# Issuing the first loads of a transfer-bound LoRA kernel ahead of the opening barrier, and its weights from a second queue

## The chip, the cores and the metric

The kernel runs on one core of one Trainium2 chip. An instruction on a queue (SP's or ACT's) issues a transfer, and the core's 16 DMA engines carry it out; the profile records each piece that an engine moves as a packet. The time is the device time of that core in microseconds (us), median of several executions. The *span* of a profile, from the first to the last instruction, is some 1.7 us shorter than the device time (163.3 against 165.0), so differences of spans can be read as differences of time.

## The reference

```python
x: (16, 2048, 256) f32   W: (256, 256)   lora_A: (256, 16)   lora_B: (16, 256)   lora_E: (16,)   scale = 1.0
x_flat = x.reshape(-1, 256)                                  # 32768 rows
y = x_flat @ W + scale * ((x_flat @ lora_A) * lora_E) @ lora_B
```

33.55 MB of x are read and 33.55 MB of y are written; the weights are 0.29 MB.

## The kernel before

The program is written engine by engine with semaphores. It folds the low-rank part into one matrix, `weff = W + A·diag(E)·B`, and then makes one matmul per tile. x comes in 8 chunks of 4 MB, each held in one of six SBUF homes of 128 partitions x 32 rows; y overwrites x in its home and is stored from there. SP issues all transfers, in one fixed order.

```python
LOAD_PIECES = {0: [8, 8, 16]}          # chunk 0 is loaded in three pieces
ORDER = ["L0", ..., "L5", "S0", "S1", "L6", "L7", "S2", ..., "S7"]
# ... cut ...
def sync_program():
    def load(pc):
        c, s, e = pc
        if c >= N_HOMES:
            sync.wait_ge(stored_of[c - N_HOMES], 16)
        sync.dma_start(out=home(c)[:, s:e, :], in_=x_chunks[c, :, s:e, :]).then_inc(loaded[pc], 16)

    load(pieces[0])                                     # 1 MB
    for name, to, of in (("w", ...), ("a", ...), ("e", ...), ("b", ...)):
        sync.dma_start(out=to[:], in_=of).then_inc(set_up_loaded[name], 16)
    for step in ORDER[:-1]:
        ...                                             # loads; stores wait for s_chunk
        if c == EARLY_AFTER:                            # after the load of chunk 1
            sync.wait_ge(s_first, 1)                    # a first small store of 2 KB
            sync.dma_start(out=y_chunks[0, :16, 0, :32], in_=home(0)[:16, 0, :32]).then_inc(s_early, 16)
# ... gpsimd: cast to bf16; tensor: transpose and multiply; scalar, vector: evict ...
nc.sync.dma_start(out=y_chunks[last], in_=home(last)[:])   # the last store
```

The whole program begins with a barrier of all engines: each drains and reports, GpSimd gathers the reports after setting some constants (at 0.5 to 0.6 us in the profile), and all are released (SP at 0.66 us).

## Time and profile before

| | before |
|---|---|
| time, median of 3 | 164.98 us (164.93 to 165.04) |
| span | 163.3 us |
| bytes moved | 67.4 MB |
| busiest compute engine (PE) | 61% of the span |
| first data packet of x | 1.97 us |
| last data packet ends | 161.83 us |

First, three lines of the page of the kernel before: busy tenths of PE and of the 16 DMA engines, and GB/s, in 40 slices of 4.1 us.

```profile
PE   0399948999999999999930089999960000000000
...
DMA  5999999998998998999999999999999999999990
GB/s 165 411 452 458 393 498 393 409 490 385 466 433 385 490 385 379 417 425 468 409 442 433 409 450 425 427 433 442 417 450 409 450 425 433 442 425 433 450 393 16
```

The DMA engines are busy in all slices but the first and the last; PE has holes, and is idle for the last quarter. GB/s jumps from slice to slice because a 32 KB packet is counted whole in one slice (the window from 58 to 60 us has a busy share of 1.39). So I read it over long windows. The last two columns of this view are the DMA engines' mean busy share and GB/s.

```profile
core 0: us, PE busy (x) PEld busy (x) DVE busy (x) ACT busy (x) POOL busy (x), PEclk, DMA share, GB/s
0.00:2.00 2.00, 0.00 (x0) 0.00 (x0) 0.00 (x0) 1.10 (x1) 0.70 (x6) 1.00 0.02 4
2.00:4.00 2.00, 0.00 (x0) 0.00 (x0) 0.00 (x0) 0.19 (x1) 0.00 (x0) 1.00 0.95 311
...
24.00:58.00 34.00, 32.57 (x268) 27.79 (x268) 25.98 (x22) 22.27 (x22) 24.74 (x24) 0.95 1.00 432
...
104.00:158.00 54.00, 16.87 (x145) 13.99 (x143) 15.95 (x14) 11.38 (x12) 9.68 (x10) 0.69 1.00 431
158.00:160.00 2.00, 0.00 (x0) 0.00 (x0) 0.00 (x0) 0.00 (x0) 0.00 (x0) 0.50 0.57 246
```

The rate is 432 GB/s while PE is busy for 33 of 34 us, and 431 from 120 to 150 us, where it is busy for 1.0 of 30: compute does not set it. 67.4 MB / 432 GB/s are 156 us of the 163.3. The only large stretch in which the DMA engines have nothing to do is the first 2 us (share 0.02). SP's issues show why.

```profile
0.94 0.38 SPq L106 DMA_DIRECT2D home<-in_x_dram  x1
1.38 0.42 SPq L115 DMA_DIRECT2D w_sb<-in_W_dram  x1
1.85 0.42 SPq L115 DMA_DIRECT2D a_sb<-in_lora_A_dram  x1
2.32 0.65 SPq L115 DMA_DIRECT2D e_sb<-in_lora_E_dram  x1
3.02 0.41 SPq L115 DMA_DIRECT2D b_sb<-in_lora_B_dram  x1
3.47 1.38 SPq L106 DMA_DIRECT2D home<-in_x_dram  x3
14.45 0.35 SPq L125 DMA_DIRECT2D out_dram<-home  x1
```

The first load is issued at 0.94 us (start, then duration), because SP has to pass the opening barrier (released at 0.66 us), and its first packet moves 1.03 us later. After that, transfers are issued well before their turn: the store of chunk 0 at 29.13 us. At the other end, SP waits 39.3 us for the last store:

```profile
SPq L272 <- DMA out_dram<-home: 39.3, 1, 39.3
```

### The profile page before, as it was taken

How to read it: one execution, taken by the hardware profiler on the slowest of the kernel's cores; microseconds unless marked ns; L12 is line 12 of the kernel's file. 1: busy time of each engine (PE TensorE's matmuls, PEld its weight loads, DVE VectorE, ACT ScalarE, POOL GpSimd, SP SyncE). 2: the span in 40 equal slices, each digit the busy share in tenths (PEclk: the TensorE clock that was granted, in tenths of full speed). 3: DMA queues.
4: the chain of work that ended last, by engine and by line, in shares of the span. 5: the costliest groups of instructions: out<-in, count | busy, mean ns of one | idle time of the engine just before them, and what ended most of it. 6: DMA issues, size and time to landing. Idle time of an engine off the chain costs nothing. (4 is left out here: it accounts for less than half of the span.)

```text
span 163.3 us, 2148 instructions
## 1 busy us (share of the span) xinstructions
PE 99.2 (61%) x778; PEld 82.6 (51%) x778; DVE 79.6 (49%) x66; ACT 66.1 (40%) x65; POOL 67.1 (41%) x70
## 2 busy tenths in 40 slices
PE   0399948999999999999930089999960000000000
PEld 0268837888888888888820078888840000000000
DVE  0115861788988888888850025888880000000000
ACT  3044732777767676777720025677720000000000
POOL 1444615777777677777500155677500000000000
PEclk9999995999999999999995557999996555555555
DMA  5999999998998998999999999999999999999990
GB/s 165 411 452 458 393 498 393 409 490 385 466 433 385 490 385 379 417 425 468 409 442 433 409 450 425 427 433 442 417 450 409 450 425 433 442 425 433 450 393 16
DMA packets 2979, 67.43 MB, mean 413 GB/s; under 512 B 528, under 2 KB 544, under 8 KB 672
## 3 DMA queue, kind: packets, MB, share of 16 engines
q1 hardware_dynamic: 2976, 67.41, 96.8%
q14 instruction: 3, 0.02, 0.0%
HBM read 33.85 MB, written 33.56 MB: 413 GB/s over the span
## 5 line engine op out<-in xcount | busy, mean ns | idle before, releaser
L181 DVE COPY home<-psum_y 128x1024 f32<-128x1024 f32 x64 | 78.4, 1225 | 32.8 <-PE psum_y L204 30.0
L151 POOL CAST stage<-home 128x1024 bf16<-128x1024 f32 x64 | 66.4, 1041 | 48.8 <-PE psum_xt L196 24.8
L162 ACT COPY xt<-psum_xt 128x1024 bf16<-128x1024 bf16 x64 | 64.8, 1012 | 52.7 <-PE psum_xt L196 52.7
L204 PE MATMUL psum_y<-weff,xt 128*128 128x256 bf16 x512 | 70.2, 283 | 1.0
L204 PEld LDWEIGHTS psum_y<-weff,xt 128*128 128x128 bf16 x512 | 48.3, 101 | 14.7 <-issue 7.1
L196 PE MATMUL psum_xt<-ident,stage 128*128 128x128 f32 x260 | 42.6, 290 | 14.0 <-PEq L189 14.0
L196 PEld LDWEIGHTS psum_xt<-ident,stage 128*128 128x128 f32 x260 | 33.2, 151 | 16.1 <-issue 15.1
L216 PE MATMUL psum_y<-ident,a_sb 128*16 128x128 f32 x2 | 0.6, 396 | 6.8 <-DMA a_sb<-in_lora_A_dram 6.8
L167 DVE TENSOR_SCALAR ate<-psum_y,e_sb 16x256 f32<-16x256 f32 x1 | 0.5, 471 | 7.5 <-PE psum_y L216 7.5
L216 PEld LDWEIGHTS psum_y<-ident,a_sb 128*16 128x16 f32 x2 | 0.1, 90 | 6.8 <-issue 6.8
L222 PE MATMUL psum_y<-b_sb,ate 16*128 16x256 f32 x4 | 2.1, 666 | 0.0
L177 DVE TENSOR_TENSOR weff<-w_sb,psum_y 128x512 bf16<-128x512 f32 x1 | 0.7, 689 | 2.4 <-PE psum_y L222 2.4
L162 ACT ACT_TABLE_LOAD x1 | 1.3, 1283 | 0.9 <-SPq L230 0.9
L222 PEld LDWEIGHTS psum_y<-b_sb,ate 16*128 16x128 f32 x4 | 1.2, 318 | 0.5 <-issue 0.3
L133 POOL MEMSET ident<- 128x128 f32 x1 | 0.2, 204 | 0.5 <-SPq L230 0.5
L135 POOL TENSOR_SCALAR_AFFINE_SELECT ident<-ident 128x128 f32<-128x128 f32 x1 | 0.3, 293 | 0.2 <-POOL ident L133 0.2
L258 POOL MEMSET const-float32-0.0<- 128x1 f32 x1 | 0.1, 98 | 0.2 <-issue 0.2
L258 POOL MEMSET const-bfloat16-1.0<- 128x1 bf16 x1 | 0.1, 101 | 0.0
L258 POOL MEMSET const-uint8-127<- 128x1 uint8 x1 | 0.1, 101 | 0.0
L258 POOL MEMSET const-float32-1.0<- 128x1 f32 x1 | 0.1, 98 | 0.0
## 6 DMA issues: line engine op xcount, KB each, us to landing
out_dram<-home SPq DMA_DIRECT2D x8, 4096.0 KB, 42.1
home<-in_x_dram SPq DMA_DIRECT2D x7, 4096.0 KB, 19.9
home<-in_x_dram SPq DMA_DIRECT2D x2, 1024.0 KB, 5.3
home<-in_x_dram SPq DMA_DIRECT2D x1, 2048.0 KB, 10.1
w_sb<-in_W_dram SPq DMA_DIRECT2D x1, 256.0 KB, 5.1
a_sb<-in_lora_A_dram SPq DMA_DIRECT2D x1, 16.0 KB, 4.9
e_sb<-in_lora_E_dram SPq DMA_DIRECT2D x1, 0.1 KB, 4.6
b_sb<-in_lora_B_dram SPq DMA_DIRECT2D x1, 16.0 KB, 4.0
```

Source lines behind the costliest of these rows:

```text
L133: gpsimd.memset(ident[:], 0.0).then_inc(s_ident, 1)
L135: gpsimd.affine_select(out=ident[:], in_=ident[:], compare_op=ALU.not_equal, fill=1.0, base=0, pattern=[[-1, P]], channel_multiplier=1,).t ...
L151: gpsimd.tensor_copy(out=stage[g % NS][:], in_=home(c)[:, b:b + CG, :]).then_inc(s_stage, 1)
L162: scalar.copy(out=xt[g % NX][:], in_=halves).then_inc(s_xt, 1)
L167: vector.tensor_scalar(out=ate[:], in0=psum_y[0][:R, :KT, :P], scalar1=e_sb[:], scalar2=float(scale), op0=ALU.mult, op1=ALU.mult,).then_in ...
L177: vector.tensor_add(out=weff[:], in0=w_sb[:], in1=psum_y[1][:, :KT, :]).then_inc(s_free, NY)
L181: vector.tensor_copy(out=home(c)[:, b:b + CG, :], in_=psum_y[g % NY][:]).then_inc(s_free, 1)
L196: ins = tensor.transpose(psum_xt[i % NT][:, b, :], words[:, b, :], ident[:])
L204: ins = tensor.matmul(psum_y[i % NY][:, b, :], xt[i % NX][:, b, t, :], weff[:, t, :], start=(t == 0), stop=(t == KT - 1),)
L216: ins = tensor.transpose(psum_y[0][:R, t, :P], a_sb[:, t, :], ident[:])
L222: ins = tensor.matmul(psum_y[1][:, t, :], ate[:, t, :], b_sb[:], start=True, stop=True)
L258: nc = _bacc.Bacc("TRN2", target_bir_lowering=False, num_devices=1)
```

## The change

The intent: let the transfers start earlier. The first x load and the load of A are moved, when the program is finalized, ahead of the opening barrier's drain on their engines. The four weight loads go to the scalar queue (ACT), so that SP's next instruction after the barrier is the second x load.

```diff
+    opening = []
+    def ahead_of_entry_barrier(nc):
+        ...   # take each instruction named in `opening` out of its block and
+        ...   # put it ahead of its engine's first Drain in the first block
+    nc.at_finalize(ahead_of_entry_barrier)
     def sync_program():
-        load(pieces[0])
-        for name, to, of in (("w", ...), ("a", ...), ("e", ...), ("b", ...)):
-            sync.dma_start(out=to[:], in_=of).then_inc(set_up_loaded[name], 16)
+        opening.append(load(pieces[0]).ins.name)
     def scalar_program():
+        for name, to, of in (("a", ...), ("e", ...), ("b", ...), ("w", ...)):
+            ins = scalar.dma_start(out=to[:], in_=of).then_inc(set_up_loaded[name], 16)
+            if name == "a":
+                opening.append(ins.ins.name)
         for g in range(N_GROUPS):
```

More of the change, by code (lines that the diff above doesn't have):

```diff
@@ L99 @@
     sync, gpsimd, scalar, vector, tensor = nc.sync, nc.gpsimd, nc.scalar, nc.vector, nc.tensor
+    opening = []
+    def ahead_of_entry_barrier(nc):
+        blocks = nc.main_func.blocks
+        for name in opening:
+            block = next(b for b in blocks if any(i.name == name for i in b.instructions))
+            ins = next(i for i in block.instructions if i.name == name)
+            assert not ins.sync_info.on_wait
+            block.instructions = [i for i in block.instructions if i.name != name]
+            first = blocks[0].instructions
+            at = next(
+                n for n, i in enumerate(first) if i.engine == ins.engine and isinstance(i, mybir.InstDrain)
+            )
+            blocks[0].instructions = first[:at] + [ins] + first[at:]
+    nc.at_finalize(ahead_of_entry_barrier)
     def sync_program():
@@ L105, in load @@
                 sync.wait_ge(stored_of[c - N_HOMES], 16)
-            sync.dma_start(out=home(c)[:, s:e, :], in_=x_chunks[c, :, s:e, :]).then_inc(loaded[pc], 16)
-        load(pieces[0])
-        for name, to, of in (
-            ("w", w_sb, W.rearrange("(q t) m -> q t m", t=KT)),
-            ("a", a_sb, lora_A.rearrange("(q t) r -> q t r", t=KT)),
-            ("e", e_sb, lora_E[:, None]),
-            ("b", b_sb, lora_B),
-        ):
-            sync.dma_start(out=to[:], in_=of).then_inc(set_up_loaded[name], 16)
+            ins = sync.dma_start(out=home(c)[:, s:e, :], in_=x_chunks[c, :, s:e, :])
+            return ins.then_inc(loaded[pc], 16)
+        opening.append(load(pieces[0]).ins.name)
         for step in ORDER[:-1]:
@@ L156, in scalar_program @@
     def scalar_program():
+        for name, to, of in (
+            ("a", a_sb, lora_A.rearrange("(q t) r -> q t r", t=KT)),
+            ("e", e_sb, lora_E[:, None]),
+            ("b", b_sb, lora_B),
+            ("w", w_sb, W.rearrange("(q t) m -> q t m", t=KT)),
+        ):
+            ins = scalar.dma_start(out=to[:], in_=of).then_inc(set_up_loaded[name], 16)
+            if name == "a":
+                opening.append(ins.ins.name)
         for g in range(N_GROUPS):
```

## The prediction

> **What bounds the kernel now.** The transfers. The page's DMA row is at 0.9 or above in every slice but the first and last; PE, the busiest engine, has 61% of the span. The windows give 432 GB/s from 24 to 58 us and 431 from 104 to 158: one flat rate[...]. 67.4 MB at 432 GB/s are 156 us of the 163.3 us span. The rest: about 2 us before the first packet (window 0 to 2 us: share 0.02), a slow first 2 us of data (311 GB/s), a dip when stores begin (60 to 62: 262 GB/s, partly made up around it), an uneven finish of the 16 DMA engines (158 to 160: share 0.57) and some 2 us of completion and closing barrier. Issuing is not the limit: the timeline of SP shows transfers issued well before their data moves (store of chunk 0: issued at 29, moves at about 59). Compute is off the path: the last output is issued at 122.7 us and SP then waits 39.3 us for its landing (SP's waits).
>
> **What the change does.**
> 1. The first x load (1 MB) goes ahead of the opening barrier. Before, SP's first step is at 0.0 us, this load's issue at 0.94, and packets begin at about 1.97: 1.03 us after issue. Now the issue should begin at 0.0 to 0.1 and packets near 1.1: 0.85 to 0.95 us earlier. The issue's 0.38 us fits before the barrier opens (GpSimd, with its memsets and drain, arrives last, at about 0.6), so the barrier should open as before or up to 0.1 us later. The 1 MB lasts 2.4 us at full rate, so the second x load, now SP's first after the barrier (near 1.0, packets near 2.1), follows without a gap. All transfers shift by about 0.9 us; this is the gain.
> 2. Four issues (0.42+0.42+0.65+0.41 = 1.9 us) leave SP for ACT. That alone buys nothing, since the rings had work meanwhile, but it keeps step 1 free of a gap. [...] the bytes are the same.
> 3. ACT issues e, b, W before its table load (1.28 us): done by about 4 us, its first copy was at 8.3. No cost.
> 4. Set-up: a_sb lands near 2.5 instead of 6.8 us, the first stage cast starts near 5 instead of 5.85, the early store's issue moves from 14.45 to about 13.4. None of it is on the path.
>
> **Prediction.** 164.98 - 0.9 = 164.1 us, 80% range 163.8 to 164.5. Faster by over 2%: 0.01; within 2%: 0.98; slower by over 2%: 0.01.
>
> **What would show it.** Step 1: first x issue at 0.0 to 0.1 us, window 0 to 2 us carrying 150 to 300 GB/s instead of 4, second x load issued near 1.0; 24 to 58 us unchanged at 432; span near 162.4. Step 2: a second queue of about 0.3 MB in the queue table. Step 4: early store about 1 us earlier.
>
> **What would make it wrong.** An issue before the barrier that takes longer than 1.03 us to its first packet; ACT's issue of A (0.42 us, begun at about 0.13) delaying the barrier; a gap after the first 1 MB; small weight packets from a second queue slowing x; a different tail, since the 16 engines finish over about 1.7 us; the dip at 60 us growing.

No term of the sum goes with them: it is still the time before less the shift of all transfers, 164.98 - 0.9 = 164.1 us. Three figures are rough or estimates. That the store of chunk 0 moves at about 59 us is an estimate (25.5 MB at 432 GB/s; by the packet records they have moved at 62.2 us). That a_sb lands near 2.5 us rests on no trace: the quickest landing in the trace before took 4.0 us. The "some 2 us" after the transfers are 1.45 us by the packet records. "The rings had work" rests on the window from 2 to 4 us, in which SP still issues weights and the DMA share is 0.95.

## The result

| | before | after |
|---|---|---|
| time, median (4 runs each) | 164.95 us (164.81 to 165.04) | 163.54 us (163.53 to 164.06) |
| ratio, 95% interval | | 0.9925 (0.9907 to 0.9944) |
| span | 163.3 us | 161.8 us |
| first data packet | 1.97 us | 1.01 us |
| last data packet ends | 161.83 us | 160.30 us |

Ratios here and below are the mean time of one kernel's fast runs over that of the other's fast runs of the same rounds, so not quite the ratio of the medians. The gain of the medians is 1.41 us where I had predicted 0.9; the time lies below my range (163.8 to 164.5).

The same lines of the changed kernel's page:

```profile
PE   0564999999999999999930099999940000000000
...
DMA  7999999999999999999999999999999999999991
GB/s 262 369 426 442 470 414 421 462 421 413 462 421 421 454 391 421 454 421 423 446 421 438 446 413 429 456 405 438 446 405 446 446 405 446 446 405 454 438 405 73
```

The difference is in the first slice, 262 GB/s instead of 165; the middle looks alike. The windows of the changed kernel:

```profile
0.00:2.00 2.00, 0.00 (x0) 0.00 (x0) 0.00 (x0) 0.00 (x0) 0.70 (x6) 1.00 0.46 119
2.00:4.00 2.00, 0.00 (x0) 0.00 (x0) 0.00 (x0) 1.28 (x1) 0.00 (x0) 1.00 1.00 410
...
24.00:58.00 34.00, 33.51 (x292) 28.52 (x290) 29.53 (x25) 24.43 (x25) 25.23 (x25) 1.00 1.01 434
...
104.00:158.00 54.00, 14.99 (x129) 12.43 (x128) 14.40 (x12) 10.12 (x10) 8.32 (x8) 0.66 1.00 431
158.00:160.00 2.00, 0.00 (x0) 0.00 (x0) 0.00 (x0) 0.00 (x0) 0.00 (x0) 0.50 0.12 49
```

The steady rate is the old one (434 and 431). The first window now carries data, and from 158 to 160 us there is little left to move. The issues of SP and ACT, from the timeline of the changed kernel (4 x loads merged in the first line; the second of them begins at 1.14 us):

```profile
0.00 2.42 SPq L125 DMA_DIRECT2D home<-in_x_dram  x4
0.12 0.39 ACTq L176 DMA_DIRECT2D a_sb<-in_lora_A_dram  x1
...
1.10 0.38 ACTq L176 DMA_DIRECT2D e_sb<-in_lora_E_dram  x1
...
1.51 0.45 ACTq L176 DMA_DIRECT2D b_sb<-in_lora_B_dram  x1
...
1.99 0.45 ACTq L176 DMA_DIRECT2D w_sb<-in_W_dram  x1
...
13.37 0.69 DVE L199 TENSOR_TENSOR weff<-w_sb,psum_y 128x512 bf16<-128x512 f32 x1 [6.53 <-DMA w_sb<-in_W_dram]
...
17.41 0.36 SPq L138 DMA_DIRECT2D out_dram<-home  x1
```

SP's wait for the last store is nearly what it was (39.7 us against 39.3): the whole row of transfers moved, its length didn't.

```profile
SPq L294 <- DMA out_dram<-home: 39.7, 1, 39.7
```

The first load is issued at 0.00 instead of 0.94 us. But the set-up came *later*, against my prediction: weff, made at 10.41 us before, waits for W until 13.37 us, and the first small store went from 14.45 to 17.41 us. The table of issues of the changed kernel (KB each, us from issue to landing) shows the cause:

```profile
w_sb<-in_W_dram ACTq DMA_DIRECT2D x1, 256.0 KB, 11.3
a_sb<-in_lora_A_dram ACTq DMA_DIRECT2D x1, 16.0 KB, 4.7
```

Before, on SP's queue, the same view had

```profile
w_sb<-in_W_dram SPq DMA_DIRECT2D x1, 256.0 KB, 5.1
a_sb<-in_lora_A_dram SPq DMA_DIRECT2D x1, 16.0 KB, 4.9
```

W's 128 pieces of 2 KB are 8 for each of the 16 DMA engines. In the packet records of the changed kernel one piece of W and one of x mostly follow each other: at first some 0.4 us from one piece of W to the next, with an 8 KB piece of x (0.31 us) between them, then 0.7 us, with a 16 KB piece (0.61 us). Of the 128 pieces of W, 55 begin where only a piece of x ends and 9 where only another piece of W does; for nearly all others both fit. Here an engine with work in both queues thus mostly took one piece from each in turn, and a small load on an otherwise short queue was still held up by large x pieces: the pieces of W begin between 6.41 and 12.17 us, before the change between 4.96 and 6.00. It did not put compute on the path, since the store of chunk 0, issued at 28.62 us, still comes behind 25.5 MB that have moved only by 61.1 us.

How then did a shift of 0.96 us become 1.41 to 1.5? I took the packet records (start and duration of every piece) and strung them into 16 chains, a packet following the one that ended where it starts. Each chain is one DMA engine; two that end within a few ns of each other can be exchanged, which leaves the set of 16 end times as it is. In us of the span:

| | first packet | mean end of the 16 engines | mean end - first packet | last engine behind the mean | last packet to end of span |
|---|---|---|---|---|---|
| before | 1.97 | 159.71 | 157.74 | 2.12 | 1.45 |
| after | 1.01 | 158.79 | 157.78 | 1.52 | 1.46 |

The difference of the spans, 1.52 us, is 0.96 (earlier first packet) - 0.04 + 0.60 (the last engine lags less) + 0.00. So the question is: does the change make the lag of the last engine smaller, or was that luck?

- **Theory A**: the weights on a second queue put the engines out of step, the dip in rate at the switch from loads to stores becomes shallower (window 60 to 62 us: 262 GB/s before, 377 after), the last engine loses less. Worth 0.5 us each time.
- **Theory B**: lag and dip scatter from run to run. The change is worth its shift, and my range ignored the scatter.
- **Theory C**: the earlier start itself makes the dip smaller.

### The profile page after: what moved, and what is told of

Its sections match the earlier page's. It is cut to its first block, busy times and chain, and to the rows that moved or that the text cites. A ratio compares the mean times of both kernels' runs of the same rounds, so it can differ in the third digit from the quotient of the medians.

```text
span 161.8 us, 2148 instructions
## 1 busy us (share of the span) xinstructions
PE 97.7 (60%) x778; PEld 80.9 (50%) x778; DVE 79.5 (49%) x66; ACT 66.1 (41%) x65; POOL 67.2 (42%) x70
## 3 DMA queue, kind: packets, MB, share of 16 engines
q1 hardware_dynamic: 2624, 67.11, 97.1%
## 5 line engine op out<-in xcount | busy, mean ns | idle before, releaser
L226 PE MATMUL psum_y<-weff,xt 128*128 128x256 bf16 x512 | 69.2, 280 | 4.7 <-PEq L211 3.7
L226 PEld LDWEIGHTS psum_y<-weff,xt 128*128 128x128 bf16 x512 | 47.4, 100 | 18.4 <-issue 11.1
L218 PE MATMUL psum_xt<-ident,stage 128*128 128x128 f32 x260 | 41.7, 286 | 11.2 <-PEq L211 11.2
L218 PEld LDWEIGHTS psum_xt<-ident,stage 128*128 128x128 f32 x260 | 32.3, 148 | 13.5 <-issue 12.6
## 6 DMA issues: line engine op xcount, KB each, us to landing
w_sb<-in_W_dram ACTq DMA_DIRECT2D x1, 256.0 KB, 11.3
```

The costliest lines, as they stand in the source:

```text
L218: ins = tensor.transpose(psum_xt[i % NT][:, b, :], words[:, b, :], ident[:])
L226: ins = tensor.matmul(psum_y[i % NY][:, b, :], xt[i % NX][:, b, t, :], weff[:, t, :], start=(t == 0), stop=(t == KT - 1),)
```

## The experiments

Eleven runs were made, on three chips, all correct. "Lag" is the last engine's end minus the mean end, as in the table above. The traces kept for e5 to e8 are of other executions than the ones read below (spans of 162.9, 162.9, 162.9 and 162.7 us, against 162.2, 163.2, 162.3 and 162.6 in the results), so figures from the packet records of these four could not be checked again; where the kept trace differs, it is said.

### e1, e5, e10: the changed kernel again

No edit; five rounds each.

> The changed kernel once more. Common part of all theories: the first packet 0.95 us earlier than before. Theory A (the weights on a second queue put the 16 DMA engines out of step, so that the dip at the switch from loads to stores is shallower and the slowest engine ends another 0.5 us earlier): ratio 0.991 to 0.992 again in nearly every run, and a dip of the packet durations from 57 to 64 us of the span of about 0.3 us per engine, against about 0.75 before. Rival B (the dip and the tail scatter from run to run, and the extra 0.5 us was luck): single runs between 163.5 and 164.5, mean ratio near 0.994, which is the 0.95 us shift alone.

> The changed kernel a third time, for its spread and another trace. Theory B (the change moves the mean end of the 16 DMA engines by the 0.95 us of the earlier first packet and nothing else; the time of a run is set by the slowest engine, whose lag behind the mean was 1.5 to 2.1 us in six traces): ratio 0.993 to 0.996, mean end of the engines minus first packet 157.5 to 157.8 us, lag of the last engine 1.5 to 2.1. Theory A (a second gain of 0.5 us from the second queue, which the repeat of before happened to hide): ratio 0.991 to 0.992, lag of the last engine 1.5 or less.

> The changed kernel beside it on the same chip. Theory B: ratio 0.993 to 0.996 against before, single runs from 163.5 to 164.3; trace: mean end minus first packet 157.5 to 157.8.

Measured: medians 163.95, 164.00 and 164.02 us; ratios 0.9948 (0.9935 to 0.9961), 0.9938 (0.9916 to 0.9959), 0.9936 (0.9924 to 0.9949). Single runs from 163.50 to 164.25 us. Mean end - first packet: 157.67, 157.74, 157.78; lag 1.89, 2.01, 2.06. The larger gain of the first comparison did not come back, as B says. A's ratio of 0.991 to 0.992 was met by none. The kept trace of e5 has a lag of 2.13, and there the mean end itself comes 158.44 us after the first packet, 0.7 us later than in all others: not only the last engine scatters.

### e4, e8: the kernel before again, for its trace

No edit; one execution each.

> The kernel before, for a second trace of it. Theory A: engines in step at the switch to stores (nearly all packets start within half a microsecond of each other) and a dip of 0.7 us or more per engine, as in the first trace. Rival B: a dip that differs from the first trace by 0.3 us or more.

> The kernel before, for a third trace. Theory B: mean end minus first packet 157.5 to 157.8, lag of the last engine anywhere from 1.5 to 2.1 us. Theory A: lag 1.9 or more, as in the two earlier traces of it.

Measured: lag 1.92 and 1.71 (A wanted 1.9 or more in e8), mean end - first packet 157.65 and 157.52; the kept trace of e8 has 1.77 and 157.58. The dip (mean excess of a packet chain from 57 to 64.5 us over packets of 1.213 us) was 0.75, 0.64 and 0.73 us per engine in the three traces of this kernel, so the dip moved less than B's "0.3 us or more", but the lag moved by 0.4 us under an unchanged program. And A's sign of engines in step was no sign: in e4 the packets' starts before the switch were spread over 0.70 us, against 0.47 in the first trace, and the dip was nearly the same.

### e2, e11: only the first x load ahead of the barrier

```diff
         opening.append(load(pieces[0]).ins.name)
+        for name, to, of in (("w", ...), ("a", ...), ("e", ...), ("b", ...)):
+            sync.dma_start(out=to[:], in_=of).then_inc(set_up_loaded[name], 16)
     def scalar_program():
-        for name, to, of in (("a", ...), ("e", ...), ("b", ...), ("w", ...)):
-            ...
```

> Only the first x load goes ahead of the opening barrier; the four weight loads stay on SP in the old order. Theory A: the shift alone, 164.95 - 0.95 = 164.0 us (ratio 0.9942), first packet near 1.0 us, engines still in step, dip of about 0.75 us per engine as before. Rival C (the earlier start itself makes the dip smaller): 163.5 us, ratio 0.991. Rival B: somewhere between, with scatter.

> Only the first x load moved, weights on SP, a second time on the same chip as the changed kernel. Theory B: within 0.15 us of the changed kernel's median. A gain from the second queue of 0.3 us or more would put it that much above.

Measured: 164.09 us, ratio 0.995 (0.9933 to 0.9966), and 163.75 us, ratio 0.9927 (0.991 to 0.9945). The changed kernel beside them had 163.95 and 164.02, so once the changed kernel was better by 0.14 and once worse by 0.27. (The second difference misses the 0.15 us that I had allowed B, on the side away from A; single runs of e11 go from 163.47 to 164.42.) The dip was 0.73 and 0.71 us, as before the change: C falls. SP's issues in e2:

```profile
0.00 0.38 SPq L125 DMA_DIRECT2D home<-in_x_dram  x1
1.00 0.33 SPq L135 DMA_DIRECT2D w_sb<-in_W_dram  x1
...
2.83 1.37 SPq L125 DMA_DIRECT2D home<-in_x_dram  x3
```

The second x load is issued at 2.83 us, before the first megabyte has gone, so the queue does not run dry: windows of e2 give 396 GB/s from 2 to 4 us.

```profile
0.00:2.00 2.00, 0.00 (x0) 0.00 (x0) 0.00 (x0) 1.04 (x1) 0.70 (x6) 1.00 0.43 102
2.00:4.00 2.00, 0.00 (x0) 0.00 (x0) 0.00 (x0) 0.24 (x1) 0.00 (x0) 1.00 0.95 396
```

Moving one load gives the whole gain, as far as this scatter lets one see; the move of the weights to ACT is not needed for it.

### e3, e6: only the queue changed

```diff
-        opening.append(load(pieces[0]).ins.name)
+        load(pieces[0])
     ...
-            if name == "a":
-                opening.append(ins.ins.name)
```

> Only the queue is changed: the four weight loads go through the scalar queue, nothing is moved ahead of the barrier. Theory A: no shift, but the smaller dip: 164.95 - 0.5 = 164.45 us (ratio 0.997), dip about 0.3 us per engine. Rivals B and C: 164.9 to 165.0, ratio 0.9995 to 1.0, dip about 0.75. In every theory W lands late (8 to 11 us after its issue) and the first early store is issued after 17 us.

> Weights on the scalar queue, nothing ahead of the barrier, a second time. Theory B: ratio 0.999 to 1.001. Theory A: 0.996 to 0.998.

Measured: ratios 0.9993 (0.998 to 1.0006) and 0.9978 (0.9958 to 0.9998). First packet at 1.94 and 1.93 us, mean end - first packet 157.50 and 157.63, lag 1.73 and 2.16, dip 0.45 and 0.80 us. In e3 W landed 9.4 us after its issue; the early store was issued at 15.79 us, not after 17 as I had expected. The first run suggests nothing; the second a gain of 0.36 us (0.2%), barely clear of 1: its ratio lies in A's range and outside B's, but with the *larger* dip. A's chain "second queue, smaller dip, faster" does not hold: e3 had the smaller dip and no clear gain, e6 the gain and a dip like that of the kernel before (0.80; 0.68 in the kept trace, where the lag is 1.98). Over both runs the queue alone is 0.25 us below the mean of the kernel before, so a gain of 0.1 to 0.4 us from the second queue without the earlier start is not excluded, and its cause would be open. Together with the earlier start I see none (e2 and e11 against e1 and e10).

### e7: one engine unloaded

What is the lag? In the traces read here, 27 to 38 packets of the stores take 1.26 to 1.32 us instead of 1.213, none of the loads from 25 to 57 us and none after 121 us does, and where the chains can be followed the slowed packets sit on one engine (in the kernel before 26 of its 28, on the chain that ends last). In the kept trace of e5 nine packets between 25 and 57 us are slowed too; none after 121 us is. 30 x 0.07 us is 2.1 us, the size of the lag. To see which engine it is:

```diff
-    nc.sync.dma_start(out=y_chunks[last], in_=home(last)[:])
+    nc.sync.dma_start(out=y_chunks[last, :, : ROWS - 4, :], in_=home(last)[:, : ROWS - 4, :])
+    for lo, hi in ((0, 120), (120, P)):
+        nc.sync.dma_start(out=y_chunks[last, lo:hi, ROWS - 4 :, :], in_=home(last)[lo:hi, ROWS - 4 :, :])
```

How the engines would share the two small transfers was an assumption of the forecast, shown by no run then, and the packet records don't number the engines. The condition from Theory B is that the engine with the slowed packets is the one that gets 32 KB less, one packet of 1.213 us.

> The changed kernel with the last store cut so that its last 4 of 32 rows go as one transfer of 120 partitions and one of 8. [...] Theory B, [...]: its lag falls by 1.2 us, the time by 0.5 to 1.2 us against the changed kernel. If it is another engine: 0 to 0.2 us slower, and the number of 4 KB packets on its chain [...] says in which group it is. Theory A has nothing to say here.

Measured: 164.13 us, ratio 0.9953 (0.9932 to 0.9974), beside 164.00 for the changed kernel, so 0.13 us slower and not faster. How the small transfers were shared can be estimated from the packet counts. In the changed kernel the 19 transfers of SP's queue have 304 packets of 4 B, 16 each; I take them as one for each engine that has a part. The page of e7 counts 2775 packets on that queue instead of 2624: 128 more are data pieces (the last store is cut in two), and 23 remain, which 15 engines for the 120 partitions and 8 for the other 8 would give, with one engine left out of the first. In the packet records, the engine that came last to the last store also ended last, at 160.79 us, and it alone was still busy with nine 4 KB pieces (so it does in the kept trace, until 161.38 us): 120 pieces over 15 engines are eight each, so by this estimate it has one piece of the other transfer too, and is not the engine left out.

### e9: seven engines loaded more

```diff
-    nc.sync.dma_start(out=y_chunks[last], in_=home(last)[:])
+    nc.sync.dma_start(out=y_chunks[last, :, : ROWS - 2, :], in_=home(last)[:, : ROWS - 2, :])
+    for lo, hi in ((0, 119), (119, P)):
+        nc.sync.dma_start(out=y_chunks[last, lo:hi, ROWS - 2 :, :], in_=home(last)[lo:hi, ROWS - 2 :, :])
```

The two conditions from Theory B are that the slow engine gets less by this edit, and that it gets more.

> The changed kernel with the last 2 rows of the last store sent as transfers of 119 and 9 partitions[...]. The bytes of all together are the same. The laggard had nine 4 KB pieces in the run with 120 and 8 partitions[...]. Theory B (the last engine alone sets the time): [...] the time falls by 0.2 to 0.5 us against the changed kernel; [...] it rises by 0.5 to 0.8 us. If the lag of one engine did not set the time but the total of the bytes did: no change within 0.2 us.

Measured: 164.80 us, ratio 0.9997 (0.9978 to 1.0016), beside 164.02 us for the changed kernel on the same chip: 0.78 us slower with the same bytes in the same order. This undoes nearly the whole gain of the change. The end of the two traces, e9 first:

```profile
158.00:159.00 1.00, 0.00 (x0) 0.00 (x0) 0.00 (x0) 0.00 (x0) 0.00 (x0) 0.50 0.50 193
159.00:160.00 1.00, 0.00 (x0) 0.00 (x0) 0.00 (x0) 0.00 (x0) 0.00 (x0) 0.50 0.16 59
160.00:162.00 2.00, 0.00 (x0) 0.00 (x0) 0.00 (x0) 0.00 (x0) 0.00 (x0) 0.50 0.05 17
```

and e10, the changed kernel beside it:

```profile
158.00:159.00 1.00, 0.00 (x0) 0.00 (x0) 0.00 (x0) 0.00 (x0) 0.00 (x0) 0.50 0.16 66
159.00:160.00 1.00, 0.00 (x0) 0.00 (x0) 0.00 (x0) 0.00 (x0) 0.00 (x0) 0.50 0.15 66
160.00:162.00 2.00, 0.00 (x0) 0.00 (x0) 0.00 (x0) 0.00 (x0) 0.00 (x0) 0.50 0.00 0
```

A share of 0.05 over 2 us of 16 engines is about one engine busy for 1.6 us: from 160 us on, e9 waits for a single engine. The packet records show it sending its last 18 pieces of 2 KB alone, 0.08 us apart, until 161.39 us, and 18 is the share of an engine that takes part in both transfers, if the first is cut into seven (17 of the 119 partitions and one of the 9). The counts fit: 2768 packets on SP's queue are 144 more than in the changed kernel, 128 data pieces and 16, which 7 + 9 engines would give. Such an engine gets 36 KB of the last two rows instead of 16 (8 pieces of 2 KB): 20 KB more, an estimated 0.76 us at 1.213 us for 32 KB, beside the 0.78 us measured. So the run ends when one engine ends, by this estimate one of seven; that was the point of B.

### All runs together

| kernel | runs | mean us | lowest to highest |
|---|---|---|---|
| before | 37 | 164.93 | 164.46 to 165.42 |
| changed (first result, e1, e5, e10) | 22 | 163.90 | 163.50 to 164.25 |
| only x ahead of the barrier (e2, e11) | 12 | 163.92 | 163.47 to 164.42 |
| only the scalar queue (e3, e6) | 11 | 164.68 | 164.40 to 164.96 |

In the eleven traces of kernels whose transfers are whole (all but e7 and e9), the mean end comes 157.50 to 157.78 us after the first packet; the lag is 1.52 to 2.16 us, 1.92 on average in the three traces before and 1.87 in the four after.

The packet records also show what the shallower dip was worth. Take as *loss* the time since the first packet, less the time in which 16 engines at 1.213 us for 32 KB would have moved the bytes moved so far:

| loss in us, after the first packet by | 12 us | 63.5 us, past the dip |
|---|---|---|
| before | 0.96 | 1.74 |
| changed, the recorded result | 1.57 | 1.79 |
| changed, e1 and e10 | 1.29 and 1.07 | 1.70 and 1.79 |
| only x ahead, e2 and e11 | 0.95 and 0.97 | 1.68 and 1.71 |
| only the queue, e3 | 1.01 | 1.50 |

The changed kernel with both moves lost up to 0.6 us more at its start, and its dip was shallower by nearly as much. So A's first step is seen in the recorded result, but it gained nothing; only the lag of the last engine differed. Why the two losses make up for each other is not shown.

No version beat the changed kernel clearly; moving the first x load alone is as fast.

## Why the prediction was right or wrong

- **The transfers bound the run: right.** The rate from 24 to 58 us was 432 GB/s before and 434 after, and 431 in both from 104 to 158 us, with PE mostly idle; the set-up came 3 us later without cost.
- **Step 1, the shift of about 0.9 us: right.** The issue came at 0.00 us and the first packet at 1.01, 0.96 us earlier. Over all runs the gain is 164.93 - 163.90 = 1.03 us, and the load alone (e2, e11) gives it. Two details were off: from 0 to 2 us the trace has 119 GB/s, not 150 to 300: the engines begin between 1.01 and 1.49 us, and their first 8 KB pieces take up to 0.89 us instead of 0.31; and the barrier opened 0.19 us later (SP released at 0.85 instead of 0.66), not "as before or up to 0.1". In e2, without the early load of A, it was released at 0.71, so about 0.14 us of the delay is ACT's issue of A and its drain. The later barrier cost nothing, because the first megabyte was still moving (window 2 to 4 us: share 1.00, 410 GB/s). A risk that I had named, small weight packets slowing x, may have come true at the start (a loss of 1.57 instead of 0.96 us by 12 us), but it was made up at the dip; e3, with the same packets on the second queue and no early start, shows no such loss (1.01), so what caused it is not shown.
- **The term of the sum that failed is "a different tail, since the 16 engines finish over about 1.7 us".** I named it as a risk and gave its change no size: 164.98 - 0.9 takes the tail as constant, with a range of 0.3 us below. (The 1.7 us was too small as well: in the trace before, the engines end from 159.03 to 161.83 us, over 2.8 us.) In the recorded comparison the lag of the last engine went from 2.12 to 1.52 us, 0.60 us on top of the shift. In seven traces of the two kernels the lag lies between 1.52 and 2.12, under unchanged programs too (1.71 to 2.12 in the kernel before, 1.52 to 2.06 in the changed one). Single runs of either kernel spread by 0.75 to almost 1 us. I had read the scatter off three runs of the kernel before, 164.93 to 165.04, which is about a ninth of what 37 runs show (164.46 to 165.42). The mean over the 22 runs, 163.90, lies inside the range predicted; the recorded median, 163.54, lies outside.
- **Step 2, the weights on ACT buy nothing by themselves: right with the earlier start** (the profile page's queue table has 0.30 MB on a second queue), since e2 and e11 keep them on SP and are as fast. My reason for the step, that it keeps step 1 free of a gap, was wrong: e2 shows no gap without it. Without the earlier start, a gain of 0.1 to 0.4 us is not excluded (e3, e6).
- **Step 4, the set-up about 1 us earlier: wrong but for the first cast**, which began at 4.67 us (near 5 predicted, 5.85 before). a_sb landed at 4.8 us instead of near 2.5, and the early store was issued at 17.41 instead of 13.4. I had treated the second queue as one that serves small transfers at once; it mostly took turns with the x pieces, and W landed 11.3 us after its issue.
- **What stays open.** Why the lag and the dip differ from run to run, and why a slower start came with a shallower dip. Why the stores of one engine, while compute runs, take 1.28 us a packet. And why three of the four recorded runs of the changed kernel came out within 0.01 us of each other at 163.53 to 163.54, where only one of 18 later runs was so low: the chips of the later runs differ from each other, and that of the first result isn't known, so a property of that chip is not excluded. The lag accounts for that run's extra 0.6 us; what made it small there isn't known.

## What to carry to other kernels

In this kernel, bound by transfers, the time before the first packet was paid in full (0.96 us less of it, 1.03 us less time over all runs): in one like it, look for what the first load waits for, and if it is only an opening barrier, issue it ahead of it; no other load has to move, as long as the next one follows before the first has gone, as in e2 (issued at 2.83 us, 396 GB/s from 2 to 4 us). The run ended with its slowest DMA engine, not with the mean (e9: 0.78 us slower with the same bytes), so take the spread from many runs before giving a range to a half-percent change, and give the tail a size. The second queue didn't serve W sooner (11.3 us to land against 5.1): beside large pieces it mostly took turns with them piece by piece, so keep set-up that is on the critical path ahead of the bulk, not beside it.
